# Silu on ScalarE, PSUM operands without copies, one ring of eight PSUM banks and operands split in place, in a hybrid attention and SSD layer

## The chip, the cores and the metric

The kernel runs on one core of a Trainium2 chip. It is one launch of one program. The metric is the device time of that launch in microseconds (us), the median of several runs. A profile is one execution recorded by the hardware profiler; its span runs from the first to the last recorded instruction. The engines are called as in the profile: PE (matrix products), PEld (its weight loads, which overlap), DVE (vector engine), ACT (scalar and activation engine), POOL (general vector engine), SP (issues the DMAs).

## The reference

One layer on x of 1024 tokens by 1024 channels, all in float32:

```
h = RMSNorm(x)
[q | k | v | z_a | xBC | z_s | dt | gates] = h @ w_in
A: differential attention, 8 heads, two softmax maps each; per-head RMS norm; * silu(z_a)
B: silu(causal depthwise conv of xBC) -> x, B, C; chunked state-space scan, 32 heads,
   4 groups, 8 chunks of 128 tokens; grouped RMSNorm(y * silu(z_s))
merged = sigmoid(g_a) * (y_a @ w_proj_attn) + sigmoid(g_s) * (y_s @ w_proj_ssd)
out = x + merged @ w_out
```

## The kernel before

**Number format.** PE multiplies in a reduced float32 format (fp32r). To keep float32 precision an operand is split into a high part (ACT copies it into fp32r) and a low part (DVE or POOL subtracts the high part), and each product is three matmuls: high by high, high by low, low by high (`steps3`). So each weight tile and each operand costs one ACT and one DVE or POOL instruction of 128x512 before PE can use it.

**Stages.** PE's large products run in this order (`bulk`, `ORDER1`):
- z projections of SSD groups 0 and 1 and the dt projection;
- the *front*: 12 pairs of conv blocks and 6 pairs of gate blocks, with the z projections of groups 2 and 3 between them. A pair is two blocks of 128 output channels by 1024 tokens, worked out in seven products in place of eight (`front_pair`). It uses three PSUM banks X, Y, Z; `ORDER` gives the seven steps and `BEFORE` what must have been taken out of a bank before a step adds to it. Step 3, the last, waits for "c22", a sum that `conv_step` puts into bank X once the conv of block half (b, 0) is through with that bank;
- the attention projections of eight heads, 8 token tiles each (`att_proj`, the tile `pma`), and beside them attention itself;
- four single gate blocks (`gates`), the three output products of four pairs each (`products`) and the last projection (`final`).

SSD chunks (`ssd_chunk`, 4 groups of 8) run beside the front and attention. In the front, SLOW us lie between two of them; after the setup of attention PACE us.

**The order.** Nothing is left to a scheduler. A planner (`Plan`) runs all tasks as generators against estimated costs and emits each instruction at its planned turn; every engine executes its own queue strictly in that order. `pl.op(engine, cost, after)` books an engine. `act` (L216), `tt` (L221), `stt` (L226), `mm` (L192), `tp` (L201), `rsqrt` (L246 to L249) and `load` (L238, issued by SP) emit and book, so most instructions of the trace carry these helpers' lines. `Slots` stand for buffers: `mms` for two PSUM banks (pool `ps_mm`: projections and a pair's Y), `trs` for six (pool `ps_tr`: all the rest, first come first served in `trs.line`), `bigs` for 17 SBUF tiles of 4 KB per partition, `mids` for 16 of 2 KB, `ws` for 9 split weight tiles.

**Places that the change touches.**
- `pair_splits`: a pair's seven weights are four raw tiles and three of their sums or differences; the four sums run on POOL (`rawf`, `s3`), each of the seven is then split: ACT, and DVE for six, POOL for the last.
- `form_evac`: four token sums of h, built from PSUM evacuations, the moving operands ("t1" to "t4") of the front.
- `conv`: four taps over a PSUM bank (one ACT, three DVE instructions, three small ones for the second half's edge), then tanh on ACT and (tanh + 1) * half on DVE, since silu(2a) = a(1 + tanh a); the constants carry the half. `z_evac` and the za part of `att_evac` do the same.
- `att_evac`: copies q and k (256 columns) and v out of the bank, squares q and k in place in PSUM, sums per head on DVE, takes (sum + eps) ** -0.5 on POOL, multiplies q and k in SBUF.
- `att_block`: the masked minimum per 512 columns of scores and a minimum of two on DVE, exp on ACT, the two maps joined on DVE, transposes, `av`; y is copied out of `av`, squared, scaled by POOL's f and by za on DVE.
- `ssd_chunk`: the matrix cb is copied from PSUM to SBUF on ACT before DVE multiplies it into the 128x1024 decay tile ab; y = pD + xn, then times z, on DVE.
- `fill`, `fill_mg`: load operands of the output products into a mid tile, split into a "form" (a bigs tile or a part of h's old place).

## Time and profile before

| | us |
|---|---|
| median of 3 runs (1749.62 to 1751.97) | 1751.63 |
| the profiled execution's own time | 1751.27 |
| its span | 1749.6 |

The mean granted clock of PE in that execution is 0.976.

| engine | busy us | instructions |
|---|---|---|
| PE | 1640.4 | 8010 |
| DVE | 1275.1 | 2463 |
| ACT | 877.1 | 2155 |
| POOL | 636.2 | 694 |

From the first instructions on a tile: the first conv pair starts at 128.0, the last gate pair ends at 625, the attention projections run from there to 1328, single gates to 1396, output products to about 1659, the last projection to the end. In the rows of the profile "out<-in" are the program's tile names, "xcount" the number of instructions, then busy us and mean ns; after the second bar stands the engine's idle time before them and what ended it. A row of waits gives total us, times, longest.

### The profile page before, as it was taken

Reading aid. Unit: us, or ns where it says so; the run is one execution under the profiler, and the core shown is the slowest. Engines: PE = TensorE matmul, PEld = TensorE weight load, DVE = VectorE, ACT = ScalarE, POOL = GpSimd, SP = SyncE. Lnnn points to the kernel's source line nnn. Section 1 sums busy time; section 2 is a strip of 40 time slices with the busy share of each in tenths; the row PEclk is TensorE's granted clock in tenths of the full one; section 3 lists DMA queues with packets and bytes.
Section 4 is the critical chain, followed back from the end, with each engine's and each line's share of the span. In section 5 each row is a group of like instructions: output and inputs, shape, how many; then the busy total and the mean of one; then the engine's idle time right before and its main releaser. Section 6 shows DMA issues by size and latency. Waiting matters only on the chain.

```text
span 1749.6 us, 24401 instructions
## 1 busy us (share of the span) xinstructions
PE 1640.4 (94%) x8010; PEld 1346.3 (77%) x8010; DVE 1275.1 (73%) x2463; ACT 877.1 (50%) x2155; POOL 636.2 (36%) x694
## 2 busy tenths in 40 slices
PE   7899999998999899999998999999899989898999
PEld 5687877876778787878887788788787867676887
DVE  7848778476863947888888888888778476888831
ACT  6424455344533537666757667666546443434410
POOL 4313332232322324343545635443545253233200
PEclk9999999998999999999999999999899999899999
DMA  5213344322442443232344524332425476787842
GB/s 195 91 61 98 104 136 127 117 88 95 125 142 87 116 120 94 68 119 68 103 138 137 168 73 121 109 115 80 126 98 174 133 258 211 266 280 252 286 159 69
DMA packets 223805, 236.48 MB, mean 135 GB/s; under 512 B 15285, under 2 KB 155326, under 8 KB 223678
## 3 DMA queue, kind: packets, MB, share of 16 engines
q1 hardware_dynamic: 223678, 234.93, 42.2%
q8 instruction: 63, 1.03, 0.3%
q14 instruction: 64, 0.52, 0.1%
HBM read 164.48 MB, written 70.39 MB: 134 GB/s over the span
## 4 chain that ended last, share of the span: by engine, by line
PE 55%; DVE 24%; ACT 8%; issue 5%; DMA 4%; POOL 3%; SPq 0%; DVEq 0%; POOLq 0%; ACTq 0%
PE pma L192 9%; PE pmz L192 7%; PE po L192 5%; PE pY L192 4%; DVE cv L226 3%; PE pX L192 3%; PE fYg L192 3%; PE av L192 2%; PE pZ L192 2%; PE fZc L192 2%; DVE p L747 2%; PE pD L192 2%; PE fXc L192 2%; PE fXg L192 2%; PE fZg L192 2%
## 5 line engine op out<-in xcount | busy, mean ns | idle before, releaser
L192 PE MATMUL pma<-w,hH 128*128 128x512 f32 x1024 | 350.8, 411 | 5.1 <-POOL w L221 3.1
L192 PEld LDWEIGHTS pma<-w,hH 128*128 128x128 f32 x1024 | 194.0, 194 | 40.5 <-POOL w L221 4.1
L221 POOL TENSOR_TENSOR rawf<-rawf,rawf 128x512 f32<-128x512 f32 x90 | 124.9, 1388 | 275.6 <-DVE wp L221 147.9
L192 PE MATMUL pma<-w,hL 128*128 128x512 f32 x512 | 210.2, 411 | 0.0
L216 ACT ACTIVATE wp<-rawf 128x512 fp32r<-128x512 f32 x180 | 110.8, 627 | 128.9 <-POOL rawf L221 27.5
L192 PE MATMUL pmz<-w,hH 128*128 128x512 f32 x512 | 163.6, 398 | 4.9 <-DVE zs L226 4.4
L221 DVE TENSOR_TENSOR wp<-rawf,wp 128x512 fp32r<-128x512 f32 x150 | 123.1, 832 | 39.3 <-ACT wp L216 37.3
L216 ACT ACTIVATE w<-raw 128x512 fp32r<-128x512 f32 (+1 forms) x122 | 74.9, 624 | 97.2 <-PE po L192 32.0
L216 ACT ACTIVATE p<-p,nm 128x256 f32<-128x256 f32 (+7 forms) x128 | 98.2, 770 | 40.0 <-DVE nm L221 27.8
L192 PEld LDWEIGHTS pmz<-w,hH 128*128 128x128 f32 x512 | 97.0, 191 | 26.2 <-DVE zs L226 5.2
L192 PEld LDWEIGHTS pma<-w,hL 128*128 128x128 f32 x512 | 99.2, 194 | 17.5
L192 PE MATMUL fYc<-ft,wp 128*128 128x512 f32 x432 | 107.5, 396 | 5.3 <-DVE fu L221 5.3
L192 PE MATMUL pmz<-w,hL 128*128 128x512 f32 x256 | 101.8, 398 | 0.0
L747 DVE CUSTOM_DVE_ANT_0 p<-sc,maskb 128x512 f32<-128x512 f32 (+2 forms) x192 | 98.6, 551 | 3.7 <-PE sc L192 3.4
L192 PEld LDWEIGHTS fYc<-ft,wp 128*128 128x128 f32 x432 | 81.6, 191 | 24.1 <-DVE fu L221 7.3
L221 POOL TENSOR_TENSOR w<-raw,w 128x512 fp32r<-128x512 f32 (+1 forms) x38 | 50.0, 1316 | 137.0 <-ACT w L216 118.2
L246 POOL TENSOR_SCALAR rs<-ss 128x4 f32<-128x4 f32 (+1 forms) x71 | 20.3, 286 | 192.3 <-DVE ss L673 161.0
L216 ACT ACTIVATE ab<-ab,nac 128x128 f32<-128x128 f32 x256 | 78.2, 390 | 4.3 <-POOL ab L1153 4.1
L221 POOL TENSOR_TENSOR wp<-rawf,wp 128x512 fp32r<-128x512 f32 x30 | 41.6, 1387 | 105.2 <-ACT wp L216 93.7
L192 PE MATMUL av<-v,at 128*128 128x128 f32 x576 | 76.4, 277 | 1.4 <-DVE at L234 0.7
L192 PEld LDWEIGHTS av<-v,at 128*128 128x128 f32 x576 | 71.9, 192 | 7.2 <-DVE at L234 1.7
L249 POOL TENSOR_TENSOR rs<-rs,mhalf 128x4 f32<-128x4 f32 (+1 forms) x71 | 72.3, 1018 | 5.9
(323 smaller groups left out, 4220.5 us busy)
## 6 DMA issues: line engine op xcount, KB each, us to landing
raw<-in_w_in_dram SPq DMA_DIRECT2D x104, 256.0 KB, 3.1
rawf<-in_w_in_dram SPq DMA_DIRECT2D x72, 256.0 KB, 4.0
ab<-act_d SPq DMA_DIRECT2D x32, 512.0 KB, 5.0
cv_d<-cv SPq DMA_DIRECT2D x48, 256.0 KB, 2.0
t_d<-ts SPq DMA_DIRECT2D x24, 512.0 KB, 2.9
z_d<-zs SPq DMA_DIRECT2D x32, 256.0 KB, 2.0
xr<-cv_d SPq DMA_DIRECT2D x32, 256.0 KB, 3.8
zc<-z_d SPq DMA_DIRECT2D x32, 256.0 KB, 3.2
```

The lines of the kernel that those rows point to most:

```text
L192: nc.tensor.matmul(o, lhsT=lhsT, rhs=rhs, start=start, stop=stop, **kw)
L216: nc.scalar.activation(o, i, f, **kw)
L221: (nc.vector if eng == "V" else nc.gpsimd).tensor_tensor(out=o, in0=a, in1=b, op=op)
L226: nc.vector.scalar_tensor_tensor(out=o, in0=a, scalar=s, in1=b, op0=op0, op1=op1)
L246: nc.gpsimd.tensor_scalar(out=dst, in0=src, scalar1=add, scalar2=None, op0=ALU.add)
L249: nc.gpsimd.tensor_tensor(out=dst, in0=dst, in1=mhalf[:, 0:cols], op=ALU.pow)
L747: nc.vector.tensor_tensor_reduce(out=p[:, j:e], in0=sc[i][:, 0:e - j], in1=maskb[:, S - n + j:S - n + e], scale=-1.0, scalar=3e38, op0=ALU ...
```

## The change

1. silu(z), silu(conv) are one ACT instruction with the function Silu; DVE's product goes, and the halves in the constants with it. (za in attention keeps Tanh.)
2. Operands stay in PSUM: q and k are multiplied straight out of the bank, y is scaled straight out of `av`, cb is read in its own bank; pD is summed in place. The banks are held accordingly longer. The joint minimum is carried from one score instruction to the next in place of a third instruction, and e1 is computed by ACT in place of DVE.
3. One ring of eight banks in place of two and six; projections and pairs go to the head of the line. c22 gets a bank of its own (fW) in place of bank X.
4. `fill` and `fill_mg` load into the low half of the form and split in place; no mid tile. The b-forms of a product start when its SSD or attention rows are there, the t-forms when the sums are. 17 forms of bigs in place of 15.
5. In front pairs three of the seven weight splits run on POOL (s3, a22, a12), in the output products none.
6. The planner: two-input operations of DVE with both inputs in SBUF and those of POOL book a shared resource "L", costs are revised, a change between Silu and Exp books 1.3 us of ACT, taps wait until DVE is nearly free (`room`), SLOW is 40 in place of 60, `form_evac` waits for all of h, an SSD group waits for all its z.

```diff
-FRONT, SLOW = 12, 60.0
+FRONT, SLOW = 12, 40.0
+ZF, ZH = {5: 2, 9: 3}, {}
...
-    def op(self, eng, cost, after):
-        s = max(self.e[eng], after, self.t)
+    def op(self, eng, cost, after, shared=False):
+
+        s = max(self.e[eng], after, self.t, self.e["L"] if shared else 0.0)
         self.e[eng] = s + cost
+        if shared:
+            self.e["L"] = s + cost
         return s + cost + HOP
...
+    def room(self, eng, ahead=0.2):
+        while self.e[eng] > self.t + ahead:
+            yield self.e[eng] - ahead
...
-    ps_mm = ctx.enter_context(tc.tile_pool(name="ps_mm", bufs=2, space=bass.MemoryType.PSUM))
-    ps_tr = ctx.enter_context(tc.tile_pool(name="ps_tr", bufs=6, space=bass.MemoryType.PSUM))
+    ps_tr = ctx.enter_context(tc.tile_pool(name="ps_tr", bufs=8, space=bass.MemoryType.PSUM))
...
-    trs, mms, qlos = Slots(6), Slots(2), Slots(2)
+    trs, qlos = Slots(8), Slots(2)
...
+        if f in (AF.Silu, AF.Exp) and f != table[0]:
+            table[0] = f
+            pl.op("A", 1.3, after)
...
+        if eng == "G":
+            return pl.op("G", 0.095 + (1.85e-3 if op == ALU.mult else 2.3e-3) * n, after, True)
+        sb = not in_ps(a, b)
+        return pl.op("V", 0.07 + 0.07 * sb + 1.042e-3 * n, after, sb)
...
-                yield from pair_splits(*raw_of.pop(i))
+                yield from pair_splits(*raw_of.pop(i), "G" if i < NFRONT else "V")
...
-        t = yield from split(s3, t3, "V")
+        t = yield from split(s3, t3, eng)
...
-        t22 = yield from split(a22, at[1], "V")
-        t = yield from split(a12, t4, "G")
+        t22 = yield from split(a22, at[1], eng)
+        t = yield from split(a12, t4, eng)
...
-        while (t, 1) not in sums12 or t < NT - 1 and (t + 1, 1) not in h_at:
+        while len(h_at) < 2 * NT:
             yield pl.t + 0.3
...
-        act(qn, pm[:, 0:256], AF.Copy, at)
-        act(v[:, t, :], pm[:, 256:384], AF.Copy, at)
+        t2 = act(qn, pm[:, 0:256], AF.Square, at)
         t1 = act(zg[:, t, :], pm[:, 384:512], AF.Tanh, at, scale=0.5)
-        t2 = act(pm[:, 0:256], pm[:, 0:256], AF.Square, t1)
+        tv = act(v[:, t, :], pm[:, 256:384], AF.Copy, at)
...
-        t2 = tt(q4, q4, rs.unsqueeze(2).to_broadcast([P, 4, 64]), ALU.mult, t2)
+        t2 = tt(qn.rearrange("p (a d) -> p a d", a=4), pm[:, 0:256].rearrange("p (a d) -> p a d", a=4),
+                rs.unsqueeze(2).to_broadcast([P, 4, 64]), ALU.mult, t2)
+        trs.give(k, max(t2, tv))
...
-                                               scale=-1.0, scalar=3e38, op0=ALU.add, op1=ALU.min, accum_out=nms[i])
+                                               scale=-1.0, scalar=nms[i - 1] if i else 3e38, op0=ALU.add, op1=ALU.min,
+                                               accum_out=nms[i])
...
-            if len(nms) > 1:
-                t1 = tt(nm, nms[0], nm, ALU.min, t1 - HOP)
...
-        stt(e1, sums[0], P * EPS, sums[0], ALU.mult, ALU.mult, at)
+        t_e = act(e1, sums[0], AF.Square, at, scale=(P * EPS) ** 0.5)
...
-        act(y, av[:, 0:P], AF.Copy, at)
         ss = tin(1, "ssv")
-        at = act(av[:, P:2 * P], av[:, 0:P], AF.Square, at, accum_out=ss)
+        at = act(y, av[:, 0:P], AF.Square, at, accum_out=ss)
...
-        at = stt(y, y, f, zg[:, qb, :], ALU.mult, ALU.mult, at)
+        at = stt(y, av[:, 0:P], f, zg[:, qb, :], ALU.mult, ALU.mult, at)
+        trs.give(k, at)
...
-            x = cell["x"]
-            cell["c22"] = at = tt(x, u, ps, ALU.add, max(at, t, cell["conv", b, 0]))
+            kw = yield from pl.get(trs, first=True)
+            w = trt(f"fW{b}")
+            cell["c22"] = at = tt(w, u, ps, ALU.add, max(at, t))
             mids.give(k, at)
-            yield from conv(b + 1, 1, x, cell, at, (trs, kx))
+            yield from conv(b + 1, 1, w, cell, at, (trs, kw))
...
-        at = act(ps, cv, AF.Tanh, at)
-        yield at
-        at = stt(cv, ps, 1.0, cv, ALU.add, ALU.mult, at)
-        cell["conv", b, h] = at
         if free:
             free[0].give(free[1], at)
+        at = act(cv, cv, AF.Silu, at)
+        cell["conv", b, h] = at
...
-        at = act(zz, pm, AF.Tanh, at, scale=0.5)
-        yield at
-        at = stt(zz, zz, 1.0, pm, ALU.add, ALU.mult, at)
-        mms.give(k, at)
+        at = act(zz, pm, AF.Silu, at)
+        trs.give(k, at)
...
+        kcb = yield from pl.get(trs, first=True)
+        pc = trt(f"pc{g}{c}")
+        mm(pc[:, 0:P], bT, cT, True, True)
+        cb, t_c = pc[:, 0:P], pe_done()
...
-        at = tt(xn, pD, xn, ALU.add, at)
+        at = tt(pD, pD, xn, ALU.add, at)
+        at = max(at - HOP, t_z)
+        yield at
+        at = tt(xn, pD, zc, ALU.mult, at)
         trs.give(k, at)
...
-    hs, fbigs, fraws = Slots(16), Slots(15), Slots(6)
+    hs, fbigs = Slots(16), Slots(NBIG)
...
-            while ("sums", c) not in ready or ready["sums", c] > pl.t:
+            while ready.get("ssd", {}).get(2 * c + 1, INF) > pl.t if c < 2 else not att_done():
                 yield pl.t + 0.5
...
+                while f[0] == "t" and ready.get(("sums", c), INF) > pl.t:
+                    yield pl.t + 0.5
...
-                    t = load(raw, src)
-                    pl.spawn(split_form(c, f, i, form, raw, km, kr, give, t), t)
+                    t = load(form[0][:, 1].bitcast(F32), src)
+                    pl.spawn(split_form(c, f, i, form, t), t)
```

136 lines of the change are left out of this document (63 added, 73 removed).

## The prediction

> **What bounds the kernel now.** I read the page's busy shares first, then the table of stretches (one row per stage), then the waits of PE.
>
> ```profile
> PE 1640.4 (94%) x8010; PEld 1346.3 (77%) x8010; DVE 1275.1 (73%) x2463; ACT 877.1 (50%) x2155; POOL 636.2 (36%) x694
> ...
> 0.00:87.50 87.50, 70.59 (x320) 53.35 (x321) 68.33 (x115) 48.32 (x105) 31.93 (x41) 0.98 0.43 143
> 87.50:131.00 43.50, 43.36 (x196) 35.51 (x195) 20.52 (x35) 9.52 (x17) 5.04 (x5) 1.00 0.18 60
> 131.00:656.00 525.00, 500.53 (x2230) 409.50 (x2229) 359.22 (x585) 227.06 (x456) 162.65 (x141) 0.98 0.37 113
> 656.00:1340.00 684.00, 641.93 (x3585) 538.46 (x3584) 568.27 (x1340) 452.51 (x1322) 324.29 (x423) 0.98 0.36 112
> 1340.00:1400.00 60.00, 56.20 (x288) 46.99 (x286) 36.76 (x86) 29.48 (x66) 17.19 (x19) 0.97 0.40 128
> 1400.00:1662.00 262.00, 243.32 (x1007) 191.89 (x1006) 202.24 (x277) 103.82 (x183) 92.57 (x65) 0.96 0.77 259
> ```
>
> A row of the second kind gives the stretch, its length, then busy us and instructions of PE, PEld, DVE, ACT and POOL, and the granted clock. PE is the bound in every stage, and the change leaves its matmuls alone. So only two things can be won: PE's idle time (length less PE busy) and the time at a lower clock (length times one minus the clock). Start: 16.9 + 1.8 us. Front (conv and gate pairs, two z projections): 24.5 + 10.5. Attention: 42.1 + 13.7, gates 3.8 + 1.8. Products: 18.7 + 10.5. The 0.97 and 0.98 are rounded, so the clock terms are good to about 3 us each. In all some 145 us. What PE waits for:
>
> ```profile
> PE pa L201 <- DVE p L226: 12.9, 14, 3.7
> PE ph L201 <- DVE x L226: 10.6, 4, 7.1
> PE fZc L192 <- DVE fXc L221: 10.5, 6, 3.0
> PE py L201 <- ACT xn L216: 9.2, 7, 4.3
> PE pya L201 <- DVE y L226: 7.5, 8, 2.0
> PE pZ L192 <- DVE hL L221: 5.9, 6, 2.9
> PE fYc L192 <- DVE fu L221: 5.3, 3, 2.8
> PE pmz L192 <- DVE zs L226: 4.4, 2, 2.6
> ```
>
> Nearly all of them end with DVE. DVE is busy 359.22 of 525 us in the front (68%) and 568.27 of 684 in attention (83%): not the bound on average, but the queue in which PE's inputs stand. **PE's gaps are DVE's delays**, and the change is worth what it takes from that queue.
>
> **The front.** Matmuls follow each other as the timeline shows:
>
> ```profile
> 130.97 2.88 PE L192 MATMUL fYc<-ft,wp 128*128 128x512 f32 x12
> 133.69 0.39 PE L192 MATMUL fXc<-hH,wp 128*128 128x512 f32 x1
> ```
>
> Twelve take 133.69 - 130.97 = 2.72 us, so a pair's 84 take 19.0 us. DVE's work for a conv pair comes from the groups of this stage (count, then busy us, mean ns):
>
> ```profile
> L221 DVE TENSOR_TENSOR wp<-rawf,wp 128x512 fp32r<-128x512 f32 x85 | 69.7, 833 | 17.9 <-ACT wp L216 17.8
> L226 DVE SCALAR_TENSOR_TENSOR cv<-fXc,cols,cv 128x511 f32<-128x511 f32 x24 | 17.8, 743 | 4.8 <-ACT cv L216 4.7
> L226 DVE SCALAR_TENSOR_TENSOR cv<-fXc,cv 128x512 f32<-128x512 f32 x24 | 16.4, 685 | 4.6 <-ACT fXc L216 4.3
> L221 DVE TENSOR_TENSOR fu<-fc,fYc 128x512 f32<-128x512 f32 x24 | 16.3, 679 | 13.9 <-PE fYc L192 13.9
> L226 DVE SCALAR_TENSOR_TENSOR zs<-zs,pmz 128x512 f32<-128x512 f32 x16 | 11.0, 686 | 38.9 <-ACT zs L216 38.9
> L226 DVE SCALAR_TENSOR_TENSOR cv<-tail,cols,cv 128x1 f32<-128x1 f32 x24 | 8.2, 344 | 0.0
> ```
>
> Twelve taps of 0.74 (8.9), six small ones of about 0.3 (1.8), four last products of 0.685 (2.7), five sums of 0.68 (3.4), six weight splits of 0.83 (5.0): 21.8 us against PE's 19.0. In conv pairs DVE is the slower engine, and catches up in gate pairs. Silu takes the four last products (2.7), the split of s3 and of a22 go to POOL (1.7): 17.4 us, below PE. Over the stage: 48 x 0.685 + 16 x 0.686 + 36 x 0.833 = 32.9 + 11.0 + 30.0 = 74 us less on DVE.
>
> SLOW from 60 to 40 brings SSD chunks forward:
>
> ```profile
> L221 DVE TENSOR_TENSOR xn<-pD,xn 128x512 f32<-128x512 f32 x7 | 4.8, 690 | 10.2 <-PE pD L192 10.1
> L221 DVE TENSOR_TENSOR ab<-ab,cb 128x1024 f32<-128x1024 f32 x7 | 9.0, 1292 | 0.0
> L221 DVE TENSOR_TENSOR xn<-pD,xn x32: 676/691/693, 267.4 to 1259.1; 128x512 f32<-128x512 f32 x32
> ```
>
> Seven chunks lie in the front now, the first at 267.4; at 40 us apart (656 - 267.4) / 40 gives about 10. A chunk costs DVE one product of 1.29, ten operations of 0.69 and two short ones, about 9 us, so 27 us move from attention into the front. That leaves 359 - 74 + 27 = 312 of 525 us, 59%.
>
> Waits: fZc <- fXc (10.5) is the last step held until c22 lies in bank x, which stood behind conv(b, 0)'s whole chain. The new bank fW cuts that: I count the row as gone. What is late next is c22's own sum, with 2.72 us of PE (step 4) to hide in; room("V") keeps a tap chain from standing in front of it. The other 24.5 us (35.0 - 10.5) I scale as a queue's delay, load / (1 - load): 0.68/0.32 = 2.1 to 0.59/0.41 = 1.4, a third less: 8 us. **Front: -18** (0 if the waits only move, -30 if all but PE's latency goes).
>
> The price on ACT. Silu and Exp may need different tables. The profiled run loads one, once (the second row is for the next paragraph but one):
>
> ```profile
> 0.78 1.28 ACT L216 ACT_TABLE_LOAD   x1 [0.78 <-PEq L1731]
> L221 POOL TENSOR_TENSOR rawf<-rawf,rawf 128x512 f32<-128x512 f32 x90 | 124.9, 1388 | 275.6 <-DVE wp L221 147.9
> ```
>
> So Exp and Tanh, both used throughout, share one. The trace can't say about Silu: none, or two loads for each of 10 chunks in the front and up to 10 around the z and dt steps, 30 x 1.28 = 38 us. ACT is busy 227 of 525 us and has room; what hurts is a weight's high part that comes 1.3 us late, and weights run about two slots (2 x 2.72 us) ahead. Between 0 and 38 I take +3.
>
> The Trainium skill (ScalarE: Activation LUTs, What ACT_TABLE_LOAD costs) speaks against the change here: each switch is a load of about 1283 ns plus a drain of about 1380. The load agrees with the trace's 1.28; no run here shows the drain. By that page the same 30 switches would be an estimated 80 us of ACT and not 38, and the term would be +6 and the time 1700.
>
> POOL takes 36 splits at about 1.39 (as rawf): 50 us more on 162.65 of 525, 41%, in a queue where the next pair's sums stand behind them; they have the two slots' 5.4 us. Two engines that work in SBUF also seem to hold each other up: the wp row has a mean of 833 against 679 for fu, which reads a PSUM bank. The moved work makes that between nothing and 50 us worse for DVE (each moved split stops it for its whole 1.39); the wp row's own excess, 36 x 0.15 = 6 us, is nearest, and leaves DVE at 60%.
>
> The Trainium skill (SBUF — State Buffer, Who interferes with whom) speaks against this move too: a DVE instruction with two SBUF inputs and a GpSimd one that reads SBUF exclude each other, and the later one waits for the whole of the other. By that page the upper end, 50 us, is possible; DVE would stand at 69% as before, the front's queue term would be 0 and the time 1705. The rows of wp agree that something of the kind happens, and not how often it would.
>
> **Start.** pmz <- zs (4.4) is PE waiting for one of two banks that ACT and then DVE empty; with Silu one 0.6 us read frees it, and there are eight banks. **-4** (0 to -6). ph <- x (10.6) is loading and normalising, unchanged. The operand sums (form_evac) now wait for the last evacuation of h: twelve operations on POOL, on DVE 12 whole ones (0.68) and 32 half-wide ones (0.42, as qk below), 22 us, moved behind the last transposes. They are due at the first fYc at 130.97, and in 87.5 to 131 DVE is busy 20.52 and POOL 5.04 of 43.5 us, which hides them; without that cover the first pair would come up to 22 us late.
>
> **Attention.** What goes from DVE, from the groups of the whole run and the view of a tile (min/median/max ns):
>
> ```profile
> L226 DVE SCALAR_TENSOR_TENSOR e<-s x64: 145/153/157, 665.8 to 1378.4; 128x1 f32<-128x1 f32 x64
> L221 DVE TENSOR_TENSOR nm<-nm 128x1 f32<-128x1 f32 x64 | 12.7, 199 | 2.2
> L221 DVE TENSOR_TENSOR qk<-qk,rs x64: 409/420/1512, 634.0 to 1334.7; 128x256 f32<-128x256 f32 x64
> L221 DVE TENSOR_TENSOR qk<-qk,rs 128x256 f32<-128x256 f32 x64 | 40.8, 638 | 12.7 <-POOL rs L249 12.5
> L226 DVE SCALAR_TENSOR_TENSOR y<-y,f,zg 128x128 f32<-128x128 f32 x64 | 34.7, 544 | 20.1 <-POOL f L249 16.9 <-ACT zg L216 2.0 <-ACT p L216 1.1
> L226 DVE SCALAR_TENSOR_TENSOR y<-y,f,zg x64: 334/351/1373, 675.8 to 1387.9; 128x128 f32<-128x128 f32 x64
> ```
>
> e: 64 x 0.153 = 9.8 (it becomes an ACT instruction). nm: 12.7. qk and y keep their place but read one operand from PSUM; their mean lies far above the median because some executions wait up to a microsecond while POOL holds something they need. The zs, fu and pD rows, which read PSUM, have means of 679 to 690 and no such tail. So I take the median: 64 x (638 - 420) = 14.0 and 64 x (544 - 351) = 12.4. With cb in PSUM the ab product (1.29) goes to about 1.2: 2. In sum 51 us, and the three chunks that left, 27: 568 - 78 = 490 of 684, 72%. ACT loses two copies per tile and gains one tiny Square, so it gets lighter; that Square stands ahead of the next Exp for about 0.2 us. The three chunks' DMAs move with them, five in and one out for each, the largest being ab's:
> ```profile
> ab<-act_d SPq DMA_DIRECT2D x32, 512.0 KB, 5.0
> ```
> They come into a stage whose DMA share is 0.37, with the next chunk's ab issued one chunk ahead: nothing.
>
> Scaled as before, 0.83/0.17 = 4.9 to 0.72/0.28 = 2.6: 47% of the 61.4 us of attention and gates go. **-29** (0 to -45: the py <- ACT xn wait has its own chain of ACT and POOL and stays).
>
> **Products, end.** In the stretch from 1400 DVE is busy 77%, and pZ <- hL waits for operands split just in time. 33 forms can stand ready in place of 31, they no longer need a mid tile, and b-forms no longer wait for the sums. The loads are as many as before, only earlier on SP's queue, and none is issued before its place is free, so nothing stands behind a waiting one for long. Against it the last split of 12 pairs returns to DVE (12 x 0.83 = 10 us). **-6** (+5 to -12). The end (84.5 of 87.6 us busy): 0.
>
> Sum: -18 + 3 - 4 - 29 - 6 = -54. The profiled execution took 1751.27 us (span 1749.6), the median of three is 1751.63: **1697**.
>
> **Rivals.**
> 1. *The wait moves to POOL or ACT* (chance 0.20). pma, y and the moved splits now lean on POOL:
> ```profile
> L249 POOL TENSOR_TENSOR rs<-rs,mhalf 128x4 f32<-128x4 f32 x64 | 67.6, 1057 | 5.3
> L246 POOL TENSOR_SCALAR rs<-ss 128x4 f32<-128x4 f32 x64 | 18.3, 286 | 175.4 <-DVE ss L673 161.0 <-DVE rec L780 12.1
> L216 ACT ACTIVATE cb<-pb x32: 250/273/294, 258.0 to 1237.3; 128x128 f32<-128x128 f32 x32
> L221 DVE TENSOR_TENSOR ab<-ab,cb x32: 1206/1217/2320, 263.6 to 1253.7; 128x1024 f32<-128x1024 f32 x32
> ```
> For it: rs waits behind 1.39 us operations. Against: POOL is under 50% everywhere. Half the gain remains: 1724. With table loads exposed (+25 in place of +3) it is much the same, 1719; both go here.
> 2. *Slower: the ring of eight runs full* (0.10). pma's bank is now held through rs and qk (0.29 + 1.06 + 0.42 = 1.8 us and their queues), av's until y, and cb keeps one from its matmul to the ab product: 5.6 us for the first chunk (258.0 to 263.6), 16.4 for the last. For it: projections lose their two banks of their own. Against: PE's list has one bank wait of note, zs. If every hold lay on PE's path, 64 x 1.8 + 64 x 1.3 (a y's add, pow and product) = 198 us; it decides at 54 / 198, a quarter exposed. With 40%: 1697 + 79 = 1776.
> 3. *More than that* (0.12): the gaps under a microsecond that no wait row names shrink too, as the plan knows DVE's real costs: of the 91 us that the forecast leaves another third goes, 1666.
> 4. *It does nothing* (0.03): Silu and PSUM reads cost what they replace, 1751.
>
> **Numbers.** Forecast 0.55 (1680 to 1712). With every term at its good end (-30, 0, -6, -45, -12) the time is 1658, at its bad end (0, +38, 0, 0, +5) 1794. The range 1660 to 1742 takes in rivals 1 and 3 and leaves out 2, 4 and a little below. A measurement tells 0.2% from no change, 3.5 us. Faster 0.87, within 0.03, slower 0.10.
>
> **What would show it.** Right: fZc <- fXc and pmz <- zs gone from PE's waits; DVE near 60% in the front and 72% in attention; qk and y with means at their medians; about 10 chunks before attention; clock nearer 1.00. Wrong: PE waiting for pma or sc banks behind qk or ab (rival 2); rows of PE waiting for POOL's wp, or dozens of table loads next to PE gaps (rival 1); DVE lighter and PE's idle time unchanged, which would mean that the order and not the load made the gaps.

## The result, and the profile after

| | before | after |
|---|---|---|
| median us (range, runs) | 1750.62 (1745.83 to 1751.97, 4) | 1657.43 (1655.36 to 1658.95, 4) |
| profiled execution: span, mean clock | 1749.6, 0.976 | 1657.2, 0.993 |

The ratio is 0.9472 [0.945, 0.9493]: 93 us faster. Forecast were 1697, that is 54 us, with a range of 1660 to 1742. The sign was right, the size was not, and the range missed by 2.6 us.

The page's busy shares of after, and the table of stretches, cut here at the first and last instruction of each stage: start, front, attention, single gates, products, last projection. Columns as in the prediction: stretch, length, busy us and instructions of PE, PEld, DVE, ACT and POOL, granted clock, DMA share, GB/s.

```profile
PE 1599.8 (97%) x8010; PEld 1328.1 (80%) x8010; DVE 1160.2 (70%) x2231; ACT 873.1 (53%) x2087; POOL 643.2 (39%) x718
...
0.00:122.60 122.60, 109.80 (x503) 85.86 (x504) 80.37 (x131) 65.59 (x128) 38.19 (x46) 1.00 0.36 118
122.60:597.80 475.20, 471.06 (x2184) 390.89 (x2183) 309.50 (x487) 254.59 (x485) 209.91 (x176) 1.00 0.42 127
597.80:1250.00 652.20, 634.82 (x3596) 535.24 (x3596) 518.24 (x1217) 407.58 (x1201) 310.48 (x429) 0.99 0.38 120
1250.00:1310.10 60.10, 60.10 (x315) 50.90 (x314) 38.92 (x81) 33.88 (x76) 15.04 (x19) 1.00 0.43 137
1310.10:1557.40 247.30, 234.17 (x1011) 190.77 (x1009) 185.35 (x278) 100.92 (x180) 63.37 (x47) 0.99 0.77 258
1557.40:1657.20 99.80, 89.83 (x409) 74.48 (x407) 27.80 (x40) 10.56 (x19) 6.17 (x4) 0.96 0.36 118
```

The same cut of before, for the two long stages (the prediction's front reached to 656 and so took in 31 us of attention):

```profile
128.30:625.10 496.80, 472.33 (x2092) 385.81 (x2091) 348.62 (x563) 218.80 (x430) 155.21 (x129) 0.98 0.37 115
625.10:1328.10 703.00, 662.95 (x3689) 556.44 (x3688) 569.84 (x1355) 452.67 (x1331) 322.69 (x427) 0.98 0.35 107
```

Idle time of PE is length less busy. Before, after and their difference are worked out from such rows of each kernel; an SSD chunk counts in the stage in which its product pD lies.

| stage | before us (idle) | after us (idle) | change | forecast |
|---|---|---|---|---|
| start | 128.3 (17.1) | 122.6 (12.8) | -5.7 | -4 |
| front | 496.8 (24.5), 6 chunks | 475.2 (4.1), 9 chunks | -21.6 | -18 + 3 |
| attention | 703.0 (40.1), 26 chunks | 652.2 (17.4), 23 chunks | -50.8 | -29, with the next row |
| single gates | 68.2 (5.8) | 60.1 (0) | -8.1 | |
| products | 262.6 (18.7) | 247.3 (13.1) | -15.3 | -6 |
| last projection | 90.7 (3.1) | 99.8 (10.0) | +9.1 | 0 |

All idle time of PE falls from 109 to 57 us. The time at a lower clock is by the mean clocks 1749.6 x 0.024 = 42 us before and 1657.2 x 0.007 = 12 us after: it falls by a larger share than the gaps do. Another 10 us lie in PE's busy time beyond the clock (1640.4 to 1599.8 is 41); matmul ends are modelled, so I do not divide these further.

PE's waits after, in us, times, longest:

```profile
PE ph L207 <- DVE x L240: 10.3, 4, 7.1
PE py L207 <- ACT xn L224: 5.7, 4, 2.4
PE po L198 <- DVE w L232: 5.5, 1, 5.5
PE pY L198 <- DVE u L232: 5.2, 2, 2.8
PE pa L207 <- DVE p L240: 4.5, 8, 1.4
...
PE fZc L198 <- DVE fW L232: 1.6, 1, 1.6
```

The waits fZc <- fXc (10.5) and pmz <- zs (4.4) are gone, pa <- p fell from 12.9 to 4.5. New is po <- w, 5.5 us in one piece: the last projection. The operations that read PSUM in place of a copy, and the price of Silu on ACT (view of a tile with min/median/max ns; groups of instructions with busy us and mean ns of one):

```profile
L232 DVE TENSOR_TENSOR qk<-pma,rs x64: 409/418/426, 608.4 to 1252.9; 128x256 f32<-128x256 f32 x64
L240 DVE SCALAR_TENSOR_TENSOR y<-av,f,zg x64: 335/345/353, 658.7 to 1309.5; 128x128 f32<-128x128 f32 x64
L224 ACT ACT_TABLE_LOAD x29 | 37.2, 1283 | 5.3 <-DVE tv L240 3.3 <-PEq L1744 0.8 <-PE pmz L198 0.8
L232 DVE TENSOR_TENSOR wp<-rawf,wp 128x512 fp32r<-128x512 f32 x68 | 56.4, 843 | 14.7 <-ACT wp L224 14.7
```

qk and y have lost their tails (1512 and 1373 ns at most before, 426 and 353 now). ACT loads a table 29 times, 37.2 us in all. The last row is that of the front alone: a weight split still takes 843 ns.

**The puzzle.** DVE's load fell about as forecast: 74 us in the front and 51 in attention were to go and 16 to come back (10 in the products, 6 in the front), 109 in all, and 1275.1 became 1160.2, 115 less. PE's time fell by nearly twice what that load was to bring. So either the load matters more than I gave it, or something other than the load made the gaps.

### The profile page after: what moved, and what is told of

It reads as the page before. It is cut to its first block, busy times and chain, and to the rows that moved or that the text cites. A ratio compares the mean times of both kernels' runs of the same rounds, so it can differ in the third digit from the quotient of the medians.

```text
span 1657.2 us, 24265 instructions
## 1 busy us (share of the span) xinstructions
PE 1599.8 (97%) x8010; PEld 1328.1 (80%) x8010; DVE 1160.2 (70%) x2231; ACT 873.1 (53%) x2087; POOL 643.2 (39%) x718
## 4 chain that ended last, share of the span: by engine, by line
PE 83%; DVE 8%; DMA 3%; ACT 2%; issue 2%; POOL 1%; SPq 0%; DVEq 0%; POOLq 0%; ACTq 0%
PE pma L198 16%; PE pmz L198 10%; PE fYc L198 6%; PE po L198 5%; PE pY L198 5%; PE fXc L198 4%; PE fZc L198 4%; PE av L198 4%; PE pZ L198 3%; PE sc L198 3%; PE pD L198 3%; PE pX L198 3%; PE fYg L198 3%; PE pg L198 3%; PE fZg L198 2%
## 5 line engine op out<-in xcount | busy, mean ns | idle before, releaser
L198 PE MATMUL pma<-w,hH 128*128 128x512 f32 x1024 | 343.9, 406 | 4.5 <-POOL w L232 2.3
L232 POOL TENSOR_TENSOR rawf<-rawf,rawf 128x512 f32<-128x512 f32 x90 | 121.4, 1349 | 253.2 <-DVE wp L232 108.4
L198 PEld LDWEIGHTS pma<-w,hH 128*128 128x128 f32 x1024 | 187.6, 190 | 39.2 <-POOL w L232 3.1
L232 DVE TENSOR_TENSOR wp<-rawf,wp 128x512 fp32r<-128x512 f32 x144 | 110.1, 784 | 35.3 <-ACT wp L224 35.2
L232 POOL TENSOR_TENSOR s<-rawf,rawf 128x512 f32<-128x512 f32 x30 | 38.8, 1293 | 128.4 <-DMA rawf<-in_w_proj_ssd_dram 50.5
L232 DVE TENSOR_TENSOR w<-raw,w 128x512 fp32r<-128x512 f32 (+1 forms) x84 | 68.5, 828 | 15.9 <-ACT w L224 15.8
```

The costliest lines, as they stand in the source:

```text
L198: nc.tensor.matmul(o, lhsT=lhsT, rhs=rhs, start=start, stop=stop, **kw)
L232: (nc.vector if eng == "V" else nc.gpsimd).tensor_tensor(out=o, in0=a, in1=b, op=op)
```

## The experiments

Three theories at the start: the *load* theory of the prediction (gaps follow DVE's busy share); the *plan* theory (the gaps come from an order planned without knowledge of collisions between DVE and POOL); and the *chain* theory (a few waits behind one long chain make them, and the edit that cuts the chain takes them). Each run's time is a median; the ratio is to the kernel before, timed beside it, with its 95% interval. Front and attention are lengths of the profiled execution, cut as above, as "front / attention"; 6 chunks lie in the front and 26 in attention where nothing else is said. The diffs are excerpts, with "..." where lines are left out. The recorded expectations number some runs: 1 is after with the old costs, 2 before with the new ones, 3 before with attention's edits, 4 after with these undone, 7 before with Silu, 8 before with bank and ring.

### Is it the plan?

**After, planned without the shared resource and with the old costs** (the instructions are those of after):

```diff
-        s = max(self.e[eng], after, self.t, self.e["L"] if shared else 0.0)
+        s = max(self.e[eng], after, self.t)
...
-        if f in (AF.Silu, AF.Exp) and f != table[0]:
-            table[0] = f
-            pl.op("A", 1.3, after)
...
```

> The changed kernel, with the planner's costs of before (no shared resource, no dearer two-input SBUF operations, nothing booked for a change of table); every instruction's kind and number stay. Theory 'load' (PE's gaps went because DVE has less to do, 115 us less busy): nearly all the gain stays, 1657 to 1670 us. Rival 'order' (the gaps went because the planned order now fits what the engines take): 1700 us or more, PE waits behind DVE come back, DVE busy stays near 1160 us. Between 1670 and 1700 both have a share.

Measured: 1668.08, ratio 0.9522 [0.9494, 0.955]; 481.5 / 657.7 (9 / 23 chunks). On top of the other edits the booked costs are worth 11 us at most, as the load theory had it; a mere re-ordering of after costs as much (10 us, below).

**Before, with the shared resource and the new costs of DVE and POOL:**

```diff
-        s = max(self.e[eng], after, self.t)
+        s = max(self.e[eng], after, self.t, self.e["L"] if shared else 0.0)
...
-            t = pl.op("G", 1.06, t)
+            t = pl.op("G", 1.06, t, True)
```

> The kernel before, with only the shared resource and the revised costs of DVE and POOL in its planner. Theory 'load': 1740 to 1755 us, as before within the scatter of any new order. Rival 'order': 1700 us or less.

Measured: 1755.02, ratio 1.002 [1.0001, 1.0039]. Nothing in sum, but very different stages; its front, its attention, one of PE's waits, and the group of qk:

```profile
123.40:656.90 533.50, 476.21 (x2093) 390.64 (x2092) 354.45 (x563) 215.82 (x430) 160.03 (x129) 0.95 0.35 107
656.90:1315.90 659.00, 643.25 (x3677) 547.66 (x3676) 566.33 (x1352) 450.23 (x1324) 323.23 (x420) 0.99 0.37 112
...
PE fZc L195 <- DVE fXc L224: 55.6, 11, 10.1
...
L224 DVE TENSOR_TENSOR qk<-qk,rs 128x256 f32<-128x256 f32 x64 | 33.5, 523 | 3.7 <-POOL rs L256 3.5
```

Attention is 44 us shorter, and with DVE busy 566.33 of 659.0 (86%, before 81%) PE idles 15.8 us in place of 40.1. A higher share with fewer gaps: the load theory fails here. Part of the collisions is planned away (qk from 638 to 523 ns). Start and gates are shorter too (123.4 and 59.1 us), but the products are 21 us longer (283.5), the last projection 4.5, and the front 37 us: there one row, fZc <- fXc, has grown from 10.5 to 55.6 us. That is the wait for c22's bank. It sent me to the front's chain.

### The front: c22's bank, the ring and Silu

**Before, with c22 in a bank of its own, from the six:**

```diff
-            while ("u", 7) not in cell or ("conv", b, 0) not in cell:
+            while ("u", 7) not in cell:
...
-            cell["c22"] = at = tt(x, u, ps, ALU.add, max(at, t, cell["conv", b, 0]))
+            kw = yield from pl.get(trs, first=True)
+            w = trt(f"fW{b}")
+            cell["c22"] = at = tt(w, u, ps, ALU.add, max(at, t))
```

> The kernel before with c22 in a bank of its own out of the six, two banks left to projections, nothing else. Theory 'c22's bank is the front's chain': front at 467 to 475 us as in run 8, total 1690 to 1725 us. Rival 'the shared ring did it': front at 485 us or more.

Measured: 1710.17, ratio 0.9755 [0.9735, 0.9774]; 478.0 / 688.8. Its front:

```profile
128.40:606.40 478.00, 464.22 (x2093) 380.45 (x2092) 351.31 (x563) 217.77 (x430) 158.95 (x129) 0.99 0.39 120
```

This bank alone shortens the front by 19 us: PE idles 13.8 us in place of 24.5, and the same matmuls keep it busy 464 us in place of 472, at a clock of 0.99 in place of 0.98. 478 us lies between what the two theories had expected. The total falls by more, 42 us; 14 of that are in attention, which this edit does not touch (see the draw of an order, below).

**Before, with that bank and one ring of eight** (`trs = Slots(8)`, every `mms` replaced by `trs`):

```diff
-    trs, mms, qlos = Slots(6), Slots(2), Slots(2)
+    trs, qlos = Slots(8), Slots(2)
```

> The kernel before with one ring of eight banks and c22 in a bank of its own, nothing else. My reading: fZc waiting for fXc (10.5 us) and pmz for zs (4.4 us) vanish, the front shortens by 10 to 20 us, 1730 to 1742 us. Rival 'ring full': attention lengthens, 1750 us or more.

Measured: 1687.05, ratio 0.9634 [0.9606, 0.9662]; 467.5 / 679.2. Its front:

```profile
127.20:594.70 467.50, 459.78 (x2092) 378.23 (x2091) 346.16 (x563) 217.87 (x430) 158.49 (x129) 1.00 0.40 122
```

Not one DVE instruction has gone (346.16 us, 563 as before), DVE's share rises to 74%, and PE's gaps fall from 24.5 to 7.7 us with the clock at 1.00. So most of the front's gaps go with DVE's load unchanged. The front is 10 us shorter than with the bank alone.

**Before, with Silu in the convs and z:**

```diff
-        at = act(ps, cv, AF.Tanh, at)
-        yield at
-        at = stt(cv, ps, 1.0, cv, ALU.add, ALU.mult, at)
...
+        at = act(cv, cv, AF.Silu, at)
...
-        at = act(zz, pm, AF.Tanh, at, scale=0.5)
-        yield at
-        at = stt(zz, zz, 1.0, pm, ALU.add, ALU.mult, at)
+        at = act(zz, pm, AF.Silu, at)
```

> The kernel before with Silu for conv and z, and nothing else (55 us less of DVE, all in start and front, some 28 table loads, not booked). Theory 'load': the front shortens by 8 to 15 us, and the whole pmz wait goes: 1730 to 1745 us. Rival 'the loads cost it': 1750 us or more. Rival 'order' (gaps of the front come from the bank of c22 and from tap chains ahead of urgent sums): the front stays within 5 us.

Measured: 1702.98, ratio 0.9733 [0.9703, 0.9763]; 467.5 / 675.6. Its front, what is left there of the wait for the bank, and a wait in the start, which is 10 us longer (138.4):

```profile
138.40:605.90 467.50, 460.47 (x2093) 378.12 (x2092) 310.39 (x498) 236.78 (x445) 157.69 (x129) 1.00 0.40 123
...
PE fZc L192 <- DVE fXc L221: 0.6, 1, 0.6
...
PE pmz L192 <- ACT zs L216: 10.6, 1, 10.6
```

Silu alone gives the front the same 29 us as bank and ring, more than either theory had expected (8 to 15 us, and at most 5): it takes the last product and one hand-over from ACT to DVE out of the chain that holds bank X, and the wait for the bank falls from 10.5 to 0.6 us. In the start zs stands in ACT's queue behind splits of the operand sums and one table load (ACT's timeline has the load at 57.54 us, zs at 58.84, and PE goes on at 59.48). So I next held that either edit is enough.

**After, on two rings (2 and 6) and with c22 in bank X again:**

```diff
-    trs, qlos = Slots(8), Slots(2)
+    trs, mms, qlos = Slots(6), Slots(2), Slots(2)
...
-            kw = yield from pl.get(trs, first=True)
-            w = trt(f"fW{b}")
-            cell["c22"] = at = tt(w, u, ps, ALU.add, max(at, t))
+            x = cell["x"]
+            cell["c22"] = at = tt(x, u, ps, ALU.add, max(at, t, cell["conv", b, 0]))
```

> The changed kernel with two and six banks as before and c22 back in bank X; Silu, splits on POOL and all else kept. Runs 7 and 8 took the same 29 us from the front, one with Silu alone, one with banks alone. Theory 'either is enough' (the front's gaps are one chain, c22 behind conv(b, 0) on a DVE that falls behind; relieving DVE or freeing the bank ends it): front at 475 to 482 us, total 1657 to 1672 us. Rival 'they add' (each has its own gaps): front at 490 us or more, total 1680 us or more.

**The same without Silu** (Tanh and DVE's product back):

> As the run before, and Silu undone too (Tanh and DVE's product, no table loads). Theory 'either is enough': now the front's gaps come back, 490 to 510 us, total 1680 to 1700 us, although the splits on POOL still spare DVE 30 us. Rival 'load' by my queue formula: DVE at some 0.69 in the front, 8 to 12 us more than in the run before. Rival 'order and costs did it': the front stays below 485 us.

Measured: 1723.22, ratio 0.9832 [0.9813, 0.985], 531.3 / 654.6; and 1751.67, ratio 0.9993 [0.9976, 1.0009], 552.9 / 653.9 (both 10 / 22 chunks). "Either is enough" fell: with Silu and without the bank the front is 56 us longer than after's. With all three undone it is 78 us longer (in both, about 4 us are one more chunk, see below), and the whole gain of the change is gone, though attention keeps its edits, the booked costs and its 654 us. PE's wait for the bank, in the first and in the second kernel:

```profile
PE fZc L200 <- DVE fXc L234: 24.7, 7, 5.9
```

```profile
PE fZc L200 <- DVE fXc L234: 42.2, 10, 8.7
```

**After, with c22 in bank X and the ring of eight kept**, and **after on two rings with the bank kept**: the diff of the first is the second half of the one above, that of the second its first half.

> The changed kernel with the ring of eight, c22 back in bank X. If c22's bank is the front's chain: front at 515 us or more, fZc waiting for fXc 20 us or more, total 1700 us or more. If the shared ring is: front below 485 us, 1670 us or less.

> The changed kernel with two and six banks again, c22 still in a bank of its own (one of the six). If c22's bank is the front's chain: front at 475 to 485 us, total 1657 to 1672 us. If the shared ring is: front at 500 us or more, 1690 us or more.

Measured: 1718.84, ratio 0.9819 [0.9776, 0.9862], 533.2 / 658.1 (10 / 22 chunks); and 1685.03, ratio 0.9622 [0.9583, 0.9662], 478.2 / 663.2 (9 / 23). The front of the first, and its wait:

```profile
120.70:653.90 533.20, 496.06 (x2217) 407.42 (x2216) 312.56 (x504) 264.52 (x506) 214.14 (x185) 0.95 0.39 119
...
PE fZc L198 <- DVE fXc L232: 23.8, 7, 5.9
```

So it is the bank: without it the front is 58 us longer. Of these, 33 are PE's idle time (37.1 us against 4.1; 23.8 stand in the wait itself) and 25 its busy time, with the clock at 0.95 in place of 1.00 and one more chunk (about 4 us). DVE is busy 59% there, less than in any quick front. The ring by itself is worth 3 us in the front (478.2 against 475.2), 5 in the start and 11 in attention. These 11 do not come again: with c22 in bank X, the ring leaves the front 2 us and attention 3.5 us longer (531.3 / 654.6 to 533.2 / 658.1), and the total falls by 4 us, 1723.22 to 1718.84; only the start is 7 us shorter there.

**After with Tanh in place of Silu:**

```diff
+        at = act(ps, cv, AF.Tanh, at)
+        yield at
+        at = stt(cv, ps, 1.0, cv, ALU.add, ALU.mult, at)
...
-        at = act(cv, cv, AF.Silu, at)
...
```

> The changed kernel with Tanh and DVE's product in place of Silu (55 us more on DVE in start and front, no table loads); ring, c22's bank and all else kept. Theory 'bank': the front has no gaps left to grow, 475 to 485 us, total 1657 to 1670 us. Rival 'load': DVE at 0.75 in the front, 490 us or more, total 1675 us or more.

Measured: 1680.05, ratio 0.96 [0.9557, 0.9643]; 487.7 / 655.3 (9 / 23 chunks). The front:

```profile
123.60:611.30 487.70, 473.56 (x2184) 390.94 (x2183) 343.59 (x556) 232.28 (x468) 211.78 (x180) 0.99 0.42 126
```

Once the bank is there, Silu is worth 12 us in the front and 23 in all. The front lies between the two expectations and the total where the load rival had it: DVE's load is not without effect. But by the queue formula a share of 70% in place of 65% would raise PE's gaps from 4.1 us to 5.3, and they are 14.1. How much of the 23 a re-ordering would bring (10 us for after) is not shown.

**Before with the new costs and the bank:**

```diff
-        s = max(self.e[eng], after, self.t)
+        s = max(self.e[eng], after, self.t, self.e["L"] if shared else 0.0)
...
+            kw = yield from pl.get(trs, first=True)
+            w = trt(f"fW{b}")
+            cell["c22"] = at = tt(w, u, ps, ALU.add, max(at, t))
```

> The kernel before with the booked costs of run 2 and c22 in a bank of its own. If run 2's longer front (533 us) was c22's bank under a plan that gives DVE more time: front at 470 to 485 us, attention near 659 us as in run 2, total 1685 to 1710 us. If the costs themselves lengthen the front: 500 us or more, total 1720 us or more.

Measured: 1708.89, ratio 0.9777 [0.9741, 0.9813]; 482.6 / 674.7. The front's row:

```profile
123.10:605.70 482.60, 465.12 (x2100) 382.67 (x2099) 357.95 (x565) 217.20 (x435) 163.89 (x129) 0.99 0.39 120
```

Under the new costs the bank takes 51 us from the front (533.5 to 482.6), under the old ones 19: with collisions booked, the plan makes a chain on a held bank dearer. By which instruction I did not isolate. Front and total came as expected for the bank, attention did not (674.7, near 659 expected).

### Attention: the edits, the plan, and the draw of an order

**Before with attention's edits alone:** q, k and y read from PSUM, the carried minimum, e1 on ACT; planner as before.

```diff
-        act(qn, pm[:, 0:256], AF.Copy, at)
+        t2 = act(qn, pm[:, 0:256], AF.Square, at)
...
-        at = stt(y, y, f, zg[:, qb, :], ALU.mult, ALU.mult, at)
+        at = stt(y, av[:, 0:P], f, zg[:, qb, :], ALU.mult, ALU.mult, at)
```

> The kernel before, with only the attention part of the change (q, k and y straight out of PSUM, minimum carried along, e1 on ACT), old planner. It takes some 50 us from DVE in attention. Theory 'load': 1715 to 1730 us (without the moved chunks 50 of the 568 us, that is 0.76 in place of 0.83 load, a third of the 61 us). Rival 'order': 1740 us or more.

Measured: 1705.01, ratio 0.9728 [0.9691, 0.9765]; 496.6 / 666.2. Attention:

```profile
624.40:1290.60 666.20, 643.85 (x3687) 543.79 (x3686) 541.96 (x1240) 424.17 (x1267) 325.63 (x432) 1.00 0.37 116
```

**After with these edits undone** (the same diff the other way, with cb's copy and pD's sum as in before):

> The changed kernel, with the copies out of PSUM in attention and in the SSD chunks put back (and e1 and the joint minimum on DVE), everything else of the change kept. DVE gets some 50 us back in attention, ACT two copies per tile. Theory 'load': 1685 us or more (half of the gain of attention gone). Rival 'order': 1657 to 1668 us, the planner finds an order for that load too.

Measured: 1670.44, ratio 0.953 [0.9498, 0.9562]; 476.2 / 656.4 (9 / 23). The edits alone bring 37 us in attention, more than either theory had, the costs alone 44 (above); undone one at a time they cost 4 and 6. They cannot both be worth 40: what one takes, the other no longer finds, or before's attention was unusually bad. Hence a control: another order of the same instructions.

**Before and after, re-ordered.** HOP is the planner's estimate of the delay between two engines; no instruction changes with it.

```diff
-HOP = 0.12
+HOP = 0.13
```

> The kernel before with the planner's hand-over time at 0.13 us in place of 0.12: the same instructions and costs, another order everywhere. Theory 'blind plan' (attention's gaps come from collisions of DVE and POOL that the old costs do not know; runs 2 and 3 both shortened attention by about 40 us, one by booking them, one by removing them): attention stays near 700 us with some 40 us of PE idle, total 1740 to 1765 us. Rival 'luck' (any new order would have done): attention at 680 us or less, or the total moves by more than 15 us.

> The changed kernel with the hand-over time at 0.13 us. Theory 'blind plan': 1650 to 1668 us. Rival 'luck': 1675 us or more. It also gives the scatter that a new order alone brings.

Measured: before 1730.96, ratio 0.9885 [0.9861, 0.9909], 493.1 / 685.3; after 1667.36, ratio 0.952 [0.9494, 0.9546], 483.8 / 651.8 (9 / 23). A changed digit in an estimate moves before by 20 us, which speaks for luck, and after by 10, as the blind plan had it. Of before's 20, attention has 17.7; its front moves by 4.

**After with 60 us between chunks in the front**, as before had it:

```diff
-FRONT, SLOW = 12, 40.0
+FRONT, SLOW = 12, 60.0
```

> The changed kernel with SLOW at 60 again. Theory 'the chunks carry their PE time with them' (three chunks of some 4.5 us): front 10 to 14 us shorter, attention as much longer, total within 8 us of 1657. Rival 'attention is DVE's' (my queue formula): attention longer by 20 us or more, total 1665 us or more.

Measured: 1650.59, ratio 0.9416 [0.939, 0.9441]: 7 us faster than after, which is within what a re-ordering moves. Front and attention:

```profile
124.00:587.70 463.70, 459.17 (x2093) 380.21 (x2092) 285.03 (x460) 232.04 (x437) 199.04 (x165) 1.00 0.40 122
587.70:1243.00 655.30, 643.40 (x3686) 544.88 (x3685) 528.28 (x1244) 424.29 (x1242) 311.08 (x428) 1.00 0.37 115
```

With 6 and 26 chunks, as in before, front and attention can be compared directly: 496.8 to 463.7 and 703.0 to 655.3. The three chunks that after brings forward lengthen its front by 11.5 us and shorten attention by 3.1.

**That kernel with old costs and attention's edits undone:**

```diff
-        s = max(self.e[eng], after, self.t, self.e["L"] if shared else 0.0)
+        s = max(self.e[eng], after, self.t)
...
-        at = stt(y, av[:, 0:P], f, zg[:, qb, :], ALU.mult, ALU.mult, at)
+        at = stt(y, y, f, zg[:, qb, :], ALU.mult, ALU.mult, at)
...
```

> The changed kernel with SLOW at 60, the old costs and all copies out of PSUM back (runs 1 and 4 undone together; 26 chunks in attention, as before the change). Theory 'either the lighter DVE or the booked collisions': attention back at 680 to 700 us, total 1680 us or more. Rival 'neither is needed, ring and splits did it': attention at 665 us or less, total 1668 us or less.

Measured: 1691.13, ratio 0.9658 [0.9619, 0.9696]; 466.6 / 689.3. Attention:

```profile
590.20:1279.50 689.30, 653.38 (x3688) 548.81 (x3687) 566.55 (x1355) 455.48 (x1332) 323.00 (x431) 0.99 0.36 112
```

Against 655.3 the two parts are worth 34 us of attention together. The orders of 26 chunks, by what attention holds:

| attention's edits | booked costs | attention us, one order each |
|---|---|---|
| no | no | 703.0 (before), 685.3, 675.5, 679.2, 688.8, 689.3 |
| yes | no | 666.2 |
| no | yes | 659.0, 674.7 |
| yes | yes | 655.3 |

Before's 703.0 is the highest of its row; the other five have a mean of 684 and lie between 676 and 689. So of the 48 us from 703.0 to 655.3 I put about 19 down to the draw of one order and 28 to 34 to the two parts. The 19 are an estimate: only the 685.3 is a pure re-ordering; the other four also carry edits of the banks, of Silu or of the front. How the 28 to 34 divide is open, since the orders of one row lie 16 to 27 us apart.

### The last projection

In after it takes 99.8 us in place of 90.7. In the kernel with 60 us between chunks, DVE splits nine operands in place (hH, hL, mg) between 1549.7 and 1559.5; behind them stands the split of a projection weight for which PE waits (timeline: begin, length, engine, instruction, and in brackets the wait before it):

```profile
1559.45 2.97 DVE L232 TENSOR_TENSOR w<-raw,w 128x512 fp32r<-128x512 f32 x3
```

```profile
1560.18 1.22 PE L198 MATMUL po<-w,hL 128*128 128x512 f32 x2 [5.54 <-DVE w L232]
```

**60 us between chunks, and the second half of the last operands held until eight of the weights are split:**

```diff
+    NWT = sum(7 if isinstance(w, list) else 1 for w in wlist)
...
-                while ready.get(("mg", ob, h), INF) > pl.t:
+                while ready.get(("mg", ob, h), INF) > pl.t or h and made[0] < NWT - KB:
```

> The changed kernel with SLOW at 60, and with fill_mg's second half (operands of tokens 512 to 1023 for the last projection) held back until the first eight weights of that projection are split. In every run with the splits in place, PE waits 5.5 us at the start of the last projection for a weight that stands on DVE behind these operands. Expected: that wait gone, the last projection at 91 to 94 us in place of 100, total 1638 to 1648 us. Rival: the wait only moves to the operands of the second half, 1648 to 1655 us.

Measured: 1643.95 (1643.42 to 1645.06), ratio 0.94 [0.9372, 0.9427], the fastest of all. The last projection, and its wait:

```profile
1548.50:1641.70 93.20, 88.11 (x409) 73.14 (x407) 26.51 (x40) 11.69 (x20) 5.77 (x4) 0.99 0.38 132
...
PE po L198 <- DVE w L232: 1.6, 2, 0.9
```

Of the 5.5 us 1.6 are left, and the stage is 6.8 us shorter than with 60 alone. The wait was not 5.5 us in every run, as the expectation says: with the old costs or in another order it was 4.0 to 4.5 us.

## Why the prediction was right about the sign and wrong about the size

**What failed: "PE's gaps are DVE's delays", and the scaling by load / (1 - load).** The load itself was well sized in sum (115 us less, 109 forecast; in the front 348.6 - 74 + 27 + 6 = 308, measured 309.5), though the products lost 16 us of DVE's work where 10 more were forecast. Its conversion into PE's time was not. Six orders of the same attention instructions give 676 to 703 us, the booked costs give 659 at 86% load, and the front goes from 24.5 to 7.7 us of gaps with no DVE instruction less. In the front the gaps went where the chain on bank X was cut and came back where it was restored. For attention the runs show that order and plan matter as well as load, and not which chain it is; that stays open.

**Front, -18 + 3 forecast, -21.6 measured, with the wrong cost for the chunks inside.** I counted the row fZc <- fXc (10.5) as gone, rightly, and scaled the rest of the gaps by a third. In fact the bank's effect was larger than its row: 19 us alone, 58 when it is taken out of after. With the gaps the granted clock changes too (0.98 before, 0.95 without the bank, 1.00 with it), a term that I had listed with 10.5 us and let follow the same third. My own sum for a conv pair, DVE's 21.8 us to 17.4 against PE's 19.0, said that the backlog would vanish and not shrink; but with bank and ring alone DVE keeps the 21.8, and 7.7 us of gaps are left, so that backlog was not what made most of them. At equal chunks the front is 33 us shorter. The three chunks cost it 11.5, since I moved DVE's 27 us and not PE's own time: 2184 matmuls in after's front against 2093 with 60 us, 471.06 against 459.17 us busy.

**The ring: a term that I left out.** It stands in the forecast only as a risk (rival 2). Its gain is 28 us by the medians (1685.03 to 1657.43; a re-ordering alone moves after by 10), and 22 in the two profiled executions: attention 11, start 5, front and products 3 each. On before with the bank it is 23 (1710.17 to 1687.05), with c22 in bank X only 4, so all but the start's part may be the draw of an order. Rival 2 did not happen: no row of PE's waits in after is for a bank held by qk, y or cb, though they hold theirs longer.

**Silu's price, +3 forecast.** 29 loads at 1283 ns, against 30 expected at most; ACT has room for them (254.59 of 475.2 us in the front), and PE's gaps there are 4.1 us in all. With Silu alone, one load does stand at the end of PE's 10.6 us wait in the start (above). The Trainium skill (ScalarE: Activation LUTs, What ACT_TABLE_LOAD costs) adds a drain of about 1380 ns to each. After's trace does not agree:

```profile
256.52 0.62 ACT L224 ACTIVATE wp<-rawf 128x512 fp32r<-128x512 f32 x1
257.16 1.28 ACT L224 ACT_TABLE_LOAD   x1
258.46 0.63 ACT L224 ACTIVATE cv<-cv 128x512 f32<-128x512 f32 x1
```

The load begins 0.02 us after the instruction before it has ended, and the next one 0.02 us after the load; so it is at every load around which ACT waits for nothing else. The +6 that the prediction estimated from it had no ground here. Silu shortened the front wherever it was tried, so its price cannot be told apart from its gain.

**POOL's splits.** Neither half of rival 1 came: the one row in which PE waits for POOL's work is pma <- w, 2.3 us in two waits, and a DVE split in the front takes 843 ns, before 833. For the collision that the Trainium skill (SBUF — State Buffer, Who interferes with whom) describes, between a DVE instruction with two SBUF inputs and a GpSimd one that reads SBUF, the rows agree: qk with both inputs in SBUF takes up to 1512 ns, with one in PSUM 426. At its upper end it was to leave the front's queue term at 0; that did not come: at equal chunks the front won 33 us with splits as long as before. The splits were not moved alone, nor were `room`, the wait of `form_evac` and the in-place forms tried by themselves.

**Attention and gates, -29 forecast, -59 measured.** The means forecast for qk and y were right to within 6 ns (418 and 345), and the edits took 570 - 528 = 42 us from DVE at equal chunks (51 forecast). About 19 us are, by the estimate above, what nobody could read from DVE's load: before had drawn a poor order. What is then left, some 40, is still more than forecast, and the plan has a share in it: I gave the booked costs no term of their own beyond rival 3. Against before's order they brought 44 us in attention and the edits 37, each alone.

**Start, -4 forecast, -5.7 measured:** pmz <- zs is gone. Which edit freed it stays open: Silu alone made a wait of that kind 10.6 us long and the start 138.4, the ring with c22's bank left it at 127.2, and the booked costs alone gave 123.4. On the changed kernel the ring is worth 5 to 7 us of it.

**Products and end, -6 forecast, -6.2 measured, partly by luck.** The products are 15.3 us shorter, but with before's operand code they also came out at 250.8 with attention's edits alone and at 252.4 with bank and ring, so some of that is the order; the last projection is 9.1 longer, which I had put at 0. The in-place splits that I took as earlier loads are DVE's work ahead of the last weights. "The end: 0" failed for want of asking what is queued ahead of the weight.

**Rivals.** Nearest was the third (more than forecast, 1666, chance 0.12): its cause, a plan that knows DVE's costs, is worth at most 11 us in after, and it leaves out the bank. The range ended at 1660 because the two large terms, front and attention, were scaled by the one formula; the sum of all good ends, 1658, stood in the text.

## What to carry to other kernels

Ask of each gap which chain it waits behind, and whether the edit cuts that chain: in this kernel's front the whole gap went then, and the lower clock with it, and no scaling by an engine's share told that. A buffer or bank that is handed on only at the end of a chain over two engines is such a place. The row of its wait is only a first guess of its price: rows of 10.5, 23.8 and 55.6 us stood for 19, 58 and 51 us of the front. Before explaining a stage of a statically planned kernel, run it once in another order of the same instructions; and when work is moved between stages, move the bound engine's time with it.

## What the runs showed of the hardware that I had not expected

- **The granted clock goes with the gaps.** In the front 2092 or 2093 matmuls kept PE busy 459.8 us with 7.7 us of gaps (clock 1.00; before with bank and ring), 464.2 with 13.8 (0.99; with the bank), 472.3 with 24.5 (0.98; before itself) and 476.2 with 57.3 (0.95; with the booked costs).
- **A change of table took 1.3 us of ACT and no more:** the load's 1283 ns and 0.02 us on each side. In after's front, where most of the 29 lie, PE's gaps are 4.1 us in all.
- **An order is worth 10 to 20 us of 1700:** the same instructions, planned with a delay estimate of 0.13 in place of 0.12, moved after by 10 and before by 20.
- **With one operand in PSUM the long executions were gone:** of 64, the longest qk took 426 ns in place of 1512, the longest y 353 in place of 1373. With attention's edits alone it was the same (426 and 352); with bank and ring alone, and both operands in SBUF, the longest were 1522 and 1406.
